# RWKV preparation: score and low-rank products issued in alternation over row halves and banks, key norms broadcast in one fp32r pass

## The chip, the core and the metric

The kernel runs on one core of a Trainium2 chip. Its metric is the device time of one execution in microseconds (us). The program is a whole small network, some 46,500 instructions long; the change touches one stage of it, about a sixth of the time.

Engines are called PE (TensorE, the matmul array), PEld (its weight loads), DVE (VectorE), ACT (ScalarE), POOL (GpSimd) and SP (SyncE, which here only issues transfers). Each engine runs its own instructions strictly in the order in which they were placed at build time; semaphores tie the engines together.

## The reference, cut to what matters

The network has two layers (attention with an mLSTM, then RWKV-7), two MLPs, a third mixer and a mixture of experts. The part that matters is the preparation of RWKV for 16 heads of 64 channels, 256 context tokens and 256 latent tokens:

```python
r, k, v = jnp.einsum('sbtd,sde->sbte', jnp.stack([xr, xk, xv]), w_rkv)
w_logit = w0 + einsum('zbtr,zrd->zbtd', tanh(einsum('btd,zdr->zbtr', xw, w1)), w2)   # z: two directions, r: 64
decay = exp(-exp(-softplus(-w_logit) - 0.5))
a = sigmoid(a0 + einsum('zbtr,zrd->zbtd', einsum('btd,zdr->zbtr', xa, a1), a2))
kk = split_heads(k * k_k);  kk = kk / max(norm(kk, axis=-1), 1e-12)       # one norm per token and head
k_dir = k[None] * (1.0 + (a - 1.0) * k_a)
...
return r, k_dir, v, decay, -kk, kk[None] * a, g
```

Then a state of 64 x 64 per head is scanned over the tokens, forward and backward (z = 0, 1). The kernel does the scan in chunks of 64 tokens: inside a chunk it needs the scores of every token against every earlier one, and the inverse of a unit triangular matrix made of them.

## The kernel before, in words

The RWKV layer (`layer1_mixer`) lies between about 860 and 1,500 us of the span. `rw_project` forms k, r, the low-rank tanh products `thw` and `tha` (rows 0 to 63 direction 0, rows 64 to 127 direction 1) and `rn`, the inverse key norms: 16 heads on 16 partitions by 512 tokens, from `rsqrt`.

After that the work runs in eight groups: context and latent segment, each with four groups `hq` of four heads. A group has two head pairs B (128 channels, one head per 64 partitions), and each pair two directions z; one (pair, direction) is called a unit below, so a group has four units and the stage 32. Group i goes through four steps:

- `rw_prep`: the elementwise coefficients of a unit (ACT and DVE), from the norms of its pair broadcast over 64 rows per head (L1261, the tile `pr`) and the low-rank products of its direction (L1271 with `w2`, L1272 with `a2`, one bank `pw` for the two). Then the scores of its two heads (L1319): `par` 0 has its operands on partitions 0 to 63, `par` 1 on 64 to 127, four chunks n each, with a masked copy to `sc` by DVE (L1322). Then four transposes (L1327) and their copy by ACT. Last, SP writes two 32 x 32 blocks per chunk to DRAM (L1332, `Ld`).
- `rw_solve`: a transfer reads `Ld` back as 128 rows (L1356, tile `L`), POOL (for group 1: DVE) inverts the triangles in 30 steps of two instructions (L1364, L1365), transfers write the result out (L1368) and back into `sc` (L1373). For groups 0 and 1 these transfers are on POOL's queue, for the others on SP's.
- `rw_merge`: joins 32-blocks to 64-blocks (L1385 transposes by DVE, L1390 and L1398 matmuls).
- `rw_scan`: four chunks in sequence, with matmuls that alternate between the directions (L1436 to L1483; L1453 has 64 x 64 operands, direction 0 on rows 0 to 63 and direction 1 on rows 64 to 127).

Groups are two ahead: the generator of `rw_prep` for group i + 2 is advanced between the chunks of `rw_scan` of group i, and `rw_solve` of group i + 2 is written after that scan. PE has two more kinds of work in the stage: the value projection (`v_product`, L242 to L244, before the first scan) and adaLN matmuls for the next block (`advance`, L337, with weights that SP loads into one buffer, L336).

The order on each engine isn't the order of the source. A scheduler at build time lists the instructions by its own estimates of their times and by when buffers come free, and each engine then keeps that order. PSUM in the stage: the tag `pa` has two banks, `pb` one, `s0` and `s1` two each for scans and merges, `ad` one. In the kernel before, `pa` serves `pr` and `pw`; `pb` serves the scores, the transposes and the coefficient product L1341.

An fp32 matmul shows in the trace as two records (a transpose or an fp32r matmul as one), each with its weight load. The operand shapes in the rows are rows*columns of the array in use, then the moving tile.

Of the kernel before, what the change touches and what calls it, by code (L numbers as in the profile page):

```python
# [23 lines left out]
F32 = mybir.dt.float32  # L24
FR = mybir.dt.float32r
I32 = mybir.dt.int32
U8 = mybir.dt.uint8
AF = mybir.ActivationFunctionType
OP = mybir.AluOpType
# [7 lines left out]
def bc(ap, shape):  # L37
    return ap.to_broadcast(shape)
# [12 lines left out]
class Kern:  # L51
# [115 lines left out]
    def put(self, parts, src, scale=None):  # L167
# [6 lines left out]
        else:  # L174
            nc.scalar.activation(h, src, AF.Copy, scale=scale)  # L175
            nc.vector.scalar_tensor_tensor(l, src, scale, parts[0], op0=OP.mult, op1=OP.subtract)  # L176

    def two(self, name, n, k, w):


        ts = [[self.big(name + i, k, w) for i in "hl"] for _ in range(n)]
        put = lambda b: tuple(t[:, b % k, :] for t in ts[b // k])
        return put, lambda b: tuple(v.bitcast(FR) for v in put(b))
# [67 lines left out]
    def setup(self):  # L251
        nc, tc, es = self.nc, self.tc, self.es
        self.cp = es.enter_context(self.pool("const", 1))
        cp = self.cp
        jp = cp.tile([128, 128], F32, name="jp")
        nc.gpsimd.iota(jp, pattern=[[1, 128]], base=0, channel_multiplier=-1, allow_small_or_imprecise_dtypes=True)
        self.ident = cp.tile([128, 128], F32, name="ident")
        nc.vector.tensor_scalar(self.ident, jp, 0.0, None, op0=OP.is_equal)
        self.negf = cp.tile([128, 128], F32, name="negf")
        nc.vector.tensor_scalar(self.negf, jp, 0.0, NEG, op0=OP.is_lt, op1=OP.mult)  # L260
        self.negb = cp.tile([128, 128], F32, name="negb")
        nc.vector.tensor_scalar(self.negb, jp, 0.0, NEG, op0=OP.is_gt, op1=OP.mult)
        self.jp = jp
        self.ones = cp.tile([128, 128], F32, name="ones")
        nc.vector.memset(self.ones, 1.0)


    def columns(self):
# [759 lines left out]
    def layer1_mixer(self):  # L1028
        nc, a = self.nc, self.a
        mc = self.modc[1]  # L1030
        with self.pool("rwp", 1) as P:
            rc = self.rw_consts(P)
            wr = a["rw_w_rkv"][0]
            w2 = P.tile([128, D], F32, name="rw_w2")
            nc.scalar.dma_start(w2, a["rw_w2"][0].rearrange("z r d -> (z r) d"))
            a2 = P.tile([128, D], F32, name="rw_a2")
            nc.scalar.dma_start(a2, a["rw_a2"][0].rearrange("z r d -> (z r) d"))
            thw = P.tile([128, 512], F32, name="thw")
            tha = P.tile([128, 512], F32, name="tha")
            rn = P.tile([16, 512], F32, name="rn")  # L1040

            S = P.tile([128, 16, 128], F32, name="rwS")
            nc.gpsimd.memset(S, 0.0)
# [55 lines left out]
    def rw_project(self, rc, mc, wr, w1, a1, g1, thw, tha, rn):  # L1099
        nc = self.nc  # L1100
# [5 lines left out]
        with self.pool("rwn", 2, side="right") as N:  # L1106
            for t in range(4):
                i = 1 if t < 2 else 0
# [3 lines left out]
        W = self.es_tmp.enter_context(self.pool("rwm", 2))  # L1112
# [34 lines left out]
        for n, wl, dst, fn in ((1, w1, thw, AF.Tanh), (4, a1, tha, AF.Copy)):  # L1147
            m = mix_all(n)
            p = self.ps("mm")
# [9 lines left out]
        m = mix_split(2)  # L1159
# [13 lines left out]
        for c in range(4):  # L1173
            wt = weights()
            for e in range(2):
                b = 2 * c + e
                p = self.ps("mm")
# [11 lines left out]
        for c in range(4):  # L1189
            wt = weights()  # L1190
            for e in range(2):
                p = self.ps("mm")
                for k in range(8):
                    self.matmul2(p[:, :256], tuple(x[:, e * 128:(e + 1) * 128] for x in wt(k)), m(k), k == 0, k == 7)
                if c + e == 0:
                    norms()
                    n2 = W.tile([16, 512], F32, name="kkn2", bufs=1)
                    nc.vector.tensor_scalar(n2, pn[:16], 1e-24, None, op0=OP.max)
                    self.rsqrt(W, rn, n2, 1.0, 0.0, "kkr")
                self.evac(rT[:, c * 2 + e, :], p[:, :256])  # L1200
        m = self.big("mix", 8, 256)
        for k in range(8):
# [32 lines left out]
    def rw_prep(self, W, rc, seg, hq, ar, w2, a2, thw, tha, rn, kT, rT, coef):  # L1235
# [21 lines left out]
        for b in range(2):  # L1257
            B = hq * 2 + b
            pr = self.ps("pa")
            for q in range(2):  # L1260
                nc.tensor.matmul(pr[q * 64:q * 64 + 64, :256], bc(self.ident[:16, 2 * B + q:2 * B + q + 1], [16, 64]),  # L1261
                                 rn[:, ts], start=True, stop=True)
            kkn = T("kkn")

            nc.vector.scalar_tensor_tensor(kkn, kT[:, B, :], rc["hkk"][:, B:B + 1], pr[:, :256],
                                           op0=OP.mult, op1=OP.mult)
            for z in range(2):
                zr = slice(z * 64, z * 64 + 64)
                rv = (lambda x: x) if z == 0 else (lambda x: x[:, ::-1])
                pw = self.ps("pa")  # L1270
                nc.tensor.matmul(pw[:, :256], w2[zr, B * 128:(B + 1) * 128], thw[zr, ts], start=True, stop=True)  # L1271
                nc.tensor.matmul(pw[:, 256:], a2[zr, B * 128:(B + 1) * 128], tha[zr, ts], start=True, stop=True)  # L1272
                lw, av = T("lw"), T("av")
                nc.scalar.activation(lw, pw[:, :256], AF.Tanh, scale=0.5, bias=rc["hw0"][:, z * 8 + B:z * 8 + B + 1])
                nc.scalar.activation(av, pw[:, 256:], AF.Tanh, scale=0.5, bias=rc["ha0"][:, z * 8 + B:z * 8 + B + 1])
# [36 lines left out]
                        nc.vector.tensor_add(cs, cs, kd[:, ::-1])  # L1312
                        self.rw_coef(rc, cs, B, coef)

                for par in range(2):
                    pr_ = slice(par * 64, par * 64 + 64)
                    p = self.ps("pb")
                    for n in range(4):
                        nc.tensor.matmul(p[:, n * NT:(n + 1) * NT], bkf[pr_, n].rearrange("p q s -> p (q s)"),  # L1319
                                         A[pr_, n, :], start=True, stop=True)  # L1320
                    u0 = z * 8 + par
                    nc.vector.tensor_mul(sc[b][:, u0:u0 + 7:2, :], p[:, :4 * NT].rearrange("p (n t) -> p n t", n=4),  # L1322
                                         bc(rc["mask"][:, z, None, :NT], [128, 4, NT]))
# [1170 lines left out]
```

## Time and profile before

| | us |
|---|---|
| median of 3 runs | 3162.48 |
| range of the runs | 3145.84 to 3168.23 |
| the profiled execution | 3164.53 |
| its span | 3162.8 |
| PE busy in the span | 2897.6 (92%) |
| DVE, ACT, POOL busy | 1500.9, 882.9, 460.1 |
| stage from the first norm broadcast to the end of the last scan | 978 to 1500 |
| mean granted TensorE clock | 0.925 |

Busy times of PE take in the modelled tail of each matmul. The chain of waits on the page follows only the last stage of the program (the experts), so the RWKV stage must be read from the trace by stretches. A granted clock of 1 is 2.4 GHz, of 0.5 is 1.2 GHz.

### The profile page before, as it was taken

Reading aid. Unit: us, or ns where it says so; the run is one execution under the profiler, and the core shown is the slowest. Engines: PE = TensorE matmul, PEld = TensorE weight load, DVE = VectorE, ACT = ScalarE, POOL = GpSimd, SP = SyncE. Lnnn points to the kernel's source line nnn. Section 1 sums busy time; section 2 is a strip of 40 time slices with the busy share of each in tenths; the row PEclk is TensorE's granted clock in tenths of the full one; section 3 lists DMA queues with packets and bytes.
Section 4 is the critical chain, followed back from the end, with each engine's and each line's share of the span. In section 5 each row is a group of like instructions: output and inputs, shape, how many; then the busy total and the mean of one; then the engine's idle time right before and its main releaser. Section 6 shows DMA issues by size and latency. Waiting matters only on the chain. (4 is left out here: it accounts for less than half of the span.)

```text
span 3162.8 us, 46512 instructions
## 1 busy us (share of the span) xinstructions
PE 2897.6 (92%) x18618; PEld 1840.2 (58%) x18618; DVE 1500.9 (47%) x3185; ACT 882.9 (28%) x1821; POOL 460.1 (15%) x714
## 2 busy tenths in 40 slices
PE   7999999999899999887999998999989998889987
PEld 4863568888757665554898866763433333333332
DVE  4436555555567557645656958551322222222122
ACT  4223343322334334323454624530000000000001
POOL 0012211111100434533101212110000000000000
PEclk9999999999997878878999968989999999999998
DMA  6326642333311234342555403368979999999994
GB/s 222 106 89 215 256 133 72 100 96 94 102 54 35 76 105 109 86 122 82 158 182 176 151 21 106 109 245 343 415 321 410 415 416 417 416 418 399 395 383 178
DMA packets 254000, 650.65 MB, mean 206 GB/s; under 512 B 68816, under 2 KB 129616, under 8 KB 215376
## 3 DMA queue, kind: packets, MB, share of 16 engines
q1 hardware_dynamic: 239552, 632.96, 54.4%
q10 hardware_dynamic: 12432, 10.45, 1.1%
q0 software_dynamic: 1792, 4.20, 0.5%
q8 instruction: 148, 2.42, 0.3%
q14 instruction: 76, 0.62, 0.1%
HBM read 639.16 MB, written 8.39 MB: 205 GB/s over the span
## 5 line engine op out<-in xcount | busy, mean ns | idle before, releaser
L2104 PE MATMUL mm<-w,xg 128*32 128x256 f32 (+1 forms) x3392 | 479.5, 486 | 0.9 <-DMA w<-in_moe_w_gu_dram 0.9
L164 DVE TENSOR_TENSOR lo<-w,hi 128x512 fp32r<-128x512 f32 (+1 forms) x330 | 297.0, 933 | 109.3 <-ACT hi L163 95.0
L163 ACT ACTIVATE hi<-w 128x512 fp32r<-128x512 f32 (+1 forms) x356 | 256.3, 770 | 235.4 <-PE tp L243 101.1
L2104 PEld LDWEIGHTS mm<-w,xg 128*32 128x32 f32 (+1 forms) x3392 | 158.7, 123 | 271.7 <-issue 232.9
L2104 PE MATMUL mm<-w,moeaT 128*32 128x256 f32 (+1 forms) x1696 | 262.9, 534 | 11.0 <-DVE moeaT L95 6.2
L2124 POOL TENSOR_TENSOR moeg<-moeg,moes 128x512 f32<-128x512 f32 (+1 forms) x39 | 41.8, 1072 | 960.4 <-ACT moes L2122 960.4
L2104 PEld LDWEIGHTS mm<-w,moeaT 128*32 128x32 f32 (+1 forms) x1696 | 90.1, 135 | 156.0 <-issue 123.1
L243 PE MATMUL mm<-mlo,hi 128*128 128x512 f32 (+1 forms) x512 | 173.3, 339 | 0.6 <-DVE mlo L173 0.6
L2147 DVE TENSOR_TENSOR moey<-mm,moegate 32x256 f32<-32x256 f32 (+1 forms) x106 | 58.0, 548 | 243.2 <-PE mm L2104 233.2
L242 PE MATMUL mm<-mhi,hi 128*128 128x512 f32 (+1 forms) x512 | 173.1, 340 | 0.0
L244 PE MATMUL mm<-mhi,lo 128*128 128x512 f32 (+1 forms) x512 | 172.3, 337 | 0.0
L2121 DVE TENSOR_SCALAR moeg<-mm 128x512 f32<-128x512 f32 (+1 forms) x39 | 23.2, 595 | 290.7 <-PE mm L2104 289.7
L2122 ACT ACTIVATE moes<-moeg 128x512 f32<-128x512 f32 (+1 forms) x39 | 21.6, 553 | 465.6 <-DVE moeg L2121 465.6
L244 PE MATMUL tp<-hi,aTl 128*128 128x512 f32 x384 | 151.6, 395 | 0.0
L243 PE MATMUL tp<-lo,aTh 128*128 128x512 f32 x384 | 151.4, 394 | 0.0
L242 PE MATMUL tp<-hi,aTh 128*128 128x512 f32 x384 | 151.0, 393 | 0.0
L164 POOL TENSOR_TENSOR lo<-w,hi 128x512 fp32r<-128x512 f32 (+1 forms) x26 | 52.8, 2032 | 370.9 <-ACT hi L163 316.5
L243 PEld LDWEIGHTS mm<-mlo,hi 128*128 128x128 f32 x512 | 96.4, 188 | 12.7 <-DVE mlo L173 1.0
L242 PEld LDWEIGHTS mm<-mhi,hi 128*128 128x128 f32 x512 | 96.0, 188 | 12.3 <-issue 0.2
L244 PEld LDWEIGHTS mm<-mhi,lo 128*128 128x128 f32 x512 | 96.4, 188 | 11.4
L1319 PE MATMUL pb<-ar,bkT 64*128 64x64 f32 (+1 forms) x512 | 96.6, 336 | 3.4 <-ACT bk L97 2.1
L2165 ACT ACTIVATE xg<-tp,modc,n 128x128 f32<-128x128 f32 x64 | 29.2, 457 | 241.2 <-DVE xg L2167 240.8
(843 smaller groups left out, 5921.1 us busy)
## 6 DMA issues: line engine op xcount, KB each, us to landing
w<-in_moe_w_gu_dram SPq DMA_DIRECT2D x256, 1024.0 KB, 17.4
w<-in_moe_w_down_dram SPq DMA_DIRECT2D x128, 1024.0 KB, 18.0
w<-in_mlp_w_dram SPq DMA_DIRECT2D x64, 1024.0 KB, 5.6
w<-in_ada_w_dram SPq DMA_DIRECT2D x48, 1024.0 KB, 5.2
w<-in_w_in_dram SPq DMA_DIRECT2D x26, 1024.0 KB, 5.3
adaw<-in_ada_w_dram SPq DMA_DIRECT2D x48, 512.0 KB, 4.1
w<-in_ab_w_in_dram SPq DMA_DIRECT2D x14, 1024.0 KB, 5.2
w<-in_rw_w_rkv_dram SPq DMA_DIRECT2D x8, 1024.0 KB, 5.3
```

The costliest lines, as they stand in the source:

```text
L163: nc.scalar.activation(h, raw, AF.Copy)
L164: (eng or nc.vector).tensor_sub(l, raw, hi)
L242: nc.tensor.matmul(out, l[0], r[0], start=start, stop=False)
L243: nc.tensor.matmul(out, l[0], r[1], start=False, stop=False)
L244: nc.tensor.matmul(out, l[1], r[0], start=False, stop=stop)
L1319: nc.tensor.matmul(p[:, n * NT:(n + 1) * NT], bkf[pr_, n].rearrange("p q s -> p (q s)"), A[pr_, n, :], start=True, stop=True)
L2104: return 8 * n, lambda p, c, l, r, s, st: nc.tensor.matmul(p[c * n:(c + 1) * n, :8 * n], l, r, start=s, stop=st, tile_position=(0, c * n))
L2121: nc.vector.tensor_scalar(g, pg[:, :w], 7.0, None, op0=OP.min)
L2122: nc.scalar.activation(s, g, AF.Sigmoid, scale=1.702)
L2124: nc.gpsimd.tensor_mul(g, g, s)
L2147: nc.vector.tensor_mul(y[:, cs], py[c * n:(c + 1) * n, :w], gate[c * n:(c + 1) * n, cs])
L2165: nc.scalar.activation(x[:, k, :], pv[:, kk, :], AF.Identity, scale=n2[:, k:k + 1], bias=sh(k))
```

## The change

There are three parts, all in the preparation.

1. **Scores.** The two heads of a unit get a bank each (`pb` for `par` 0, now `pa` for `par` 1), and the chunk loop is outside: the source alternates row half 0 and row half 1, chunk by chunk.
2. **Low-rank products.** Both directions' banks are taken at once (`pws`), and the four matmuls of a pair are written as w2 of direction 0, w2 of direction 1, a2 of direction 0, a2 of direction 1.
3. **Norms.** `rn` has 48 rows: a rounded part on rows 0 to 15, zeros, and the remainder on rows 32 to 47 (new helper `stack`, once). Per pair POOL spreads two columns of a constant into a 48 x 128 selector, and one fp32r matmul (L1274 of the changed kernel) makes both heads' rows. It takes the place of two fp32 matmuls of 16 rows by 64 columns.

```diff
+    def stack(self, t, rows):
+        nc = self.nc
+        nc.gpsimd.tensor_scalar(t.bitcast(FR), bc(self.ones[:48, 0:1], list(t.shape)), 0.0, None, op0=OP.mult)
+        nc.scalar.activation(t[0:16].bitcast(FR), rows, AF.Copy)
+        nc.vector.tensor_sub(t[32:48].bitcast(FR), rows, t[0:16])
...
+        self.two16 = cp.tile([48, 16], F32, name="two16")
+        nc.vector.tensor_add(self.two16.bitcast(FR), self.ident[:48, 0:16], self.ident[:48, 32:48])
...
-            rn = P.tile([16, 512], F32, name="rn")
+            rn = P.tile([48, 512], F32, name="rn")
...
-                    self.rsqrt(W, rn, n2, 1.0, 0.0, "kkr")
+                    self.rsqrt(W, n2, n2, 1.0, 0.0, "kkr")
+                    self.stack(rn, n2)
...
             pr = self.ps("pa")
-            for q in range(2):
-                nc.tensor.matmul(pr[q * 64:q * 64 + 64, :256], bc(self.ident[:16, 2 * B + q:2 * B + q + 1], [16, 64]),
-                                 rn[:, ts], start=True, stop=True)
+            sel = T("hsel", 128)[:48]
+            nc.gpsimd.tensor_scalar(sel.rearrange("p (q m) -> p q m", q=2).bitcast(FR),
+                                    bc(self.two16[:, 2 * B:2 * B + 2, None], [48, 2, 64]), 1.0, None, op0=OP.mult)
+            nc.tensor.matmul(pr[:, :256], sel.bitcast(FR), rn[:, ts].bitcast(FR), start=True, stop=True)
...
+            pws = [self.ps("pa") for _ in range(2)]
+            for i, (m, th) in enumerate(((w2, thw), (a2, tha))):
+                for z in range(2):
+                    zr = slice(z * 64, z * 64 + 64)
+                    nc.tensor.matmul(pws[z][:, i * 256:(i + 1) * 256], m[zr, B * 128:(B + 1) * 128], th[zr, ts],
+                                     start=True, stop=True)
             for z in range(2):
-                zr = slice(z * 64, z * 64 + 64)
...
-                pw = self.ps("pa")
-                nc.tensor.matmul(pw[:, :256], w2[zr, B * 128:(B + 1) * 128], thw[zr, ts], start=True, stop=True)
-                nc.tensor.matmul(pw[:, 256:], a2[zr, B * 128:(B + 1) * 128], tha[zr, ts], start=True, stop=True)
+                pw = pws[z]
...
-                for par in range(2):
-                    pr_ = slice(par * 64, par * 64 + 64)
-                    p = self.ps("pb")
-                    for n in range(4):
+                ps2 = [self.ps(tag) for tag in ("pb", "pa")]
+                for n in range(4):
+                    for par, p in enumerate(ps2):
+                        pr_ = slice(par * 64, par * 64 + 64)
                         nc.tensor.matmul(p[:, n * NT:(n + 1) * NT], bkf[pr_, n].rearrange("p q s -> p (q s)"),
                                          A[pr_, n, :], start=True, stop=True)
+                for par, p in enumerate(ps2):
                     u0 = z * 8 + par
```

The scheduler places the whole program anew, so the order on the engines changes beyond these lines, but, one small DVE instruction of the setup aside, only inside the RWKV stage. Three places follow. Lines of the changed kernel stand 10 to 17 lower in its source: L1335 is the score product, L1344 the transposes, L1284 the low-rank products, L1274 the norms, L249 to L251 the value projection.

On PE, the scores of the first unit, before: two runs of four matmuls into the one bank `pb`, with other work between.

```order
L1319 MATMUL pb<-ar,bkT 128x64 x4
L1261 MATMUL pa<-rn,ident 64x256 x2
L242 MATMUL s_7462<-hl,mix_6864 128x512
L243 MATMUL s_7462<-hl,mix_6864 128x512
L1319 MATMUL pb<-ar,bkT 128x64 x4
L244 MATMUL s_7462<-hl,mix_6865 128x512
```

The same unit in the changed kernel, with the matmul ahead of it and the transposes behind it:

```order
L251 MATMUL s_7471<-hl,mix_6870 128x512
L1335 MATMUL pb<-ar,bkT 128x64
L1335 MATMUL pa<-ar,bkT 128x64
L1335 MATMUL pb<-ar,bkT 128x64
L1335 MATMUL pa<-ar,bkT 128x64
L1335 MATMUL pb<-ar,bkT 128x64
L1335 MATMUL pa<-ar,bkT 128x64
L1335 MATMUL pb<-ar,bkT 128x64
L1335 MATMUL pa<-ar,bkT 128x64
L1344 MATMUL pb<-ident,bkT 128x128 x4
```

Here the eight matmuls alternate. 21 of the 32 units stand like this.

On PE, the fourth unit of the changed kernel (banks numbered; its scores are in `pa_7095` and `pb_7094`, `hsel` is the new selector):

```order
L1335 MATMUL pa_7054<-ar_6921,bkT_7046 128x64
L1335 MATMUL pa_7095<-ar_6921,bkT_7087 128x64 x2
L1344 MATMUL pb_7065<-ident_60,bkT_7046 128x128 x4
L1335 MATMUL pa_7095<-ar_6921,bkT_7087 128x64 x2
L1274 MATMUL pa_7198<-rn_5972,hsel_7199 128x256
L1335 MATMUL pb_7094<-ar_6921,bkT_7087 128x64 x4
L1284 MATMUL pa_7204<-thw_5970,rw_w2_5966 128x256
L1284 MATMUL pa_7205<-thw_5970,rw_w2_5966 128x256
```

Its two halves are not alternated: the half in `pa` goes ahead, around the third unit's transposes, and the half in `pb` follows. 11 units, all of direction 1, stand in this manner. The two directions' low-rank products stand next to each other.

On SP's queue, the read of group 4's blocks, before (`Ld_8902` is group 4's, `Ld_9480` group 5's):

```order
L1332 DMA Ld_8902<-sc_8900 32x8x32 x2
L336 DMA adaw_7702<-in_ada_w_2_dram 128x1024
L1332 DMA Ld_9480<-sc_9477 32x8x32
L1356 DMA L_9319<-Ld_8902 64x1024 x2
L1332 DMA Ld_9480<-sc_9477 32x8x32
```

and in the changed kernel (`Ld_8915` is group 4's, `Ld_9495` group 5's):

```order
L1349 DMA Ld_8915<-sc_8913 32x8x32 x4
L346 DMA adaw_7711<-in_ada_w_2_dram 128x1024 x2
L1373 DMA L_9334<-Ld_8915 64x1024 x2
L346 DMA adaw_7711<-in_ada_w_2_dram 128x1024
L1349 DMA Ld_9495<-sc_9492 32x8x32 x2
```

The read of group 4 stood behind a write of the next group's first unit; now it stands behind two adaLN loads. The same holds for group 5.

## Rows read from the trace of the kernel before

**Rows 1.** Page, part 1: busy time, share of the span, instructions of each engine.

```profile
PE 2897.6 (92%) x18618; PEld 1840.2 (58%) x18618; DVE 1500.9 (47%) x3185; ACT 882.9 (28%) x1821; POOL 460.1 (15%) x714
```

**Rows 2.** Stretches of the RWKV stage: length, busy time per engine, clock, DMA share, GB/s.

```profile
978.00:1018.00 40.00, 38.01 (x153) 26.61 (x150) 24.46 (x65) 15.62 (x43) 0.00 (x0) 0.66 0.05 12
1097.00:1142.00 45.00, 45.00 (x576) 29.95 (x575) 21.19 (x54) 20.46 (x53) 4.48 (x8) 0.81 0.36 106
1195.00:1244.00 49.00, 47.24 (x440) 28.56 (x440) 34.34 (x85) 17.43 (x44) 25.30 (x64) 0.76 0.35 91
1301.00:1360.00 59.00, 54.48 (x616) 36.50 (x614) 35.09 (x86) 18.97 (x49) 24.93 (x64) 0.82 0.30 76
1360.00:1500.00 140.00, 115.52 (x1526) 74.82 (x1522) 78.22 (x179) 49.15 (x117) 56.22 (x132) 0.83 0.35 101
```

**Rows 3.** Timeline of POOL: start, us, instruction, idle before and its releaser (solves).

```profile
1257.04 0.60 POOL L1358 COPY Tr<-L 64x512 f32<-64x512 f32 x1 [31.49 <-DMA L<-Ld]
...
1367.77 0.83 POOL L1358 COPY Tr<-L 64x512 f32<-64x512 f32 x1 [26.07 <-DMA L<-Ld]
...
1419.40 0.60 POOL L1358 COPY Tr<-L 64x512 f32<-64x512 f32 x1 [21.55 <-DMA L<-Ld]
...
1446.67 0.12 POOL L1367 MEMSET Tr<- 64x16 f32 x1
```

**Rows 4.** Timeline of SP's queue, around the read of group 4's blocks.

```profile
1243.47 0.89 SPq L1332 DMA_DIRECT2D Ld<-sc  x2
...
1252.19 2.20 SPq L1356 DMA_DIRECT2D L<-Ld  x2
```

**Rows 5.** Line L1385 (DVE, merges): what ended DVE's idle time (us, times).

```profile
  DMA sc<-Td: 15.5, 5
```

**Rows 6.** Timeline of PE: four score matmuls of one head, at either clock.

```profile
987.77 1.10 PE L1319 MATMUL pb<-ar,bkT 64*128 64x64 f32 x8 [0.21 <-DVE bkT L1301]
...
996.20 1.80 PE L1319 MATMUL pb<-ar,bkT 64*128 64x64 f32 x8
```

**Rows 7.** Timeline of PE: scan matmuls that alternate between the row halves.

```profile
1108.09 1.12 PE L1453 MATMUL s<-Xss,sc 64*64 64x64 f32 x16
```

**Rows 8.** Timeline of PE: low-rank products, one direction alone, then two together.

```profile
978.96 0.70 PE L1271 MATMUL pa<-thw,rw_w 64*128 64x256 f32 x2
979.49 0.59 PE L1272 MATMUL pa<-tha,rw_a 64*128 64x256 f32 x2
...
985.06 0.71 PE L1271 MATMUL pa<-thw,rw_w 64*128 64x256 f32 x4
985.59 0.61 PE L1272 MATMUL pa<-tha,rw_a 64*128 64x256 f32 x4
```

**Rows 9.** Timeline of PE: norm broadcast of a pair (x4) and of one head (x2).

```profile
978.38 0.65 PE L1261 MATMUL pa<-rn,ident 16*64 16x256 f32 x4
...
1002.24 1.11 PE L1261 MATMUL pa<-rn,ident 16*64 16x256 f32 x2
```

**Rows 10.** Timeline of PE: fp32r matmuls of 256 columns, back to back.

```profile
957.83 0.28 PE L242 MATMUL mm<-mix,hi 128*128 128x256 f32 x1
957.95 0.28 PE L243 MATMUL mm<-mix,hi 128*128 128x256 f32 x1
```

**Rows 11.** Groups on POOL, 1000 to 1460: busy us, mean ns, idle before.

```profile
L1364 POOL TENSOR_TENSOR Tm<-Tr,L 128x120 f32<-128x120 f32 x21 | 8.9, 426 | 1.6
```

**Rows 12.** Tile rn: duration ns min/median/max, first and last start us.

```profile
L115 DVE TENSOR_TENSOR rn<-rn,kkr_t x1: 678/678/678, 956.7 to 956.7; 16x512 f32<-16x512 f32 x1
```

**Rows 13.** Timeline of PE: value projection matmuls, back to back.

```profile
980.58 0.39 PE L244 MATMUL s<-hl,mix 128*128 128x512 f32 x1
980.81 0.40 PE L242 MATMUL s<-hl,mix 128*128 128x512 f32 x1
```

**Rows 14.** Line L1322 (DVE, masked copies): what ended DVE's idle time (us, times).

```profile
  PE pb L1319: 44.4, 39
```

**Rows 15.** Timeline of ACT: the first read of a `pw` bank.

```profile
980.12 0.48 ACT L1274 ACTIVATE lw<-pa,rw_hw 128x256 f32<-128x256 f32 x1 [1.26 <-PE pa L1272]
```

## The prediction

> **What bounds the kernel now.** I began with the page's first part: PE is busy for 92% of the span [rows 1]. That mean covers stages with other limits, and the page's chain covers only the experts, so I cut the RWKV stage into stretches. In four of them PE is busy for 38.01 of 40, 45.00 of 45, 47.24 of 49 and 54.48 of 59 us, while DVE has 21 to 35 us and the granted clock lies between 0.66 and 0.82 [rows 2]. These are the stretches in which the units of groups 0, 2, 4 and 6 are prepared.
>
> Between them something else paces. POOL idles before each solve until `L` lands: 31.49 us before group 4's, 26.07 before group 6's, 21.55 before group 7's [rows 3]. A solve takes about 27 us (1419.40 to 1446.67), and DVE in turn waits for the solved blocks to come back, 15.5 us in 5 waits [rows 5]. So I read one chain through the stage: PE prepares a group; its blocks go out and in by DMA; POOL solves; the blocks return; the merge starts; PE scans and prepares the group after next. The last links are solve 7, its merge and its scan, to 1500. From 1360 on PE is busy for 115.52 of 140 us [rows 2]. **PE time counts only where it lies in the four PE-paced stretches**; elsewhere it opens idle time that nothing asks for.
>
> **The change part by part.**
>
> *Scores.* Four matmuls of one head take 1.10 us at 2.4 GHz and 1.80 at 1.2 GHz [rows 6], some 0.2 of it the tail of the last; a unit has two such runs. What alternation does to them is not shown with this line, but nearly: the scan's 64-row matmuls that alternate between row halves finish 16 records in 1.12 us [rows 7], the time in which eight of the scores' finish. I take one run for the price of two: an alternated unit saves 0.9 us (1.10 less the tail) at the high clock and 1.7 at the low, 1.3 in a mixture. The bounds are nothing (the scan's pairs differ in columns too) and 1.8. By the order, 21 units alternate, of them three in group 0, three in group 2, two each in groups 4 and 6. For the other 11 I count nothing.
>
> *Low-rank products.* One direction takes 1.1 us (978.96 to the end of the second row), two that happen to stand together 1.14 (985.06 to the end of the fourth row) [rows 8]. That is the pattern of the change, already in the trace: the row halves run side by side. Saved per pair: 1.1 us at the high clock, about double at the low; where the trace paired them already, nothing. In program order those four instructions were w2, a2, w2, a2, yet the trace has all four w2 records before the a2 records. The Trainium skill's "TensorE: Matmul & The Clock Gate", section "Part 3: Packing small matmuls — row/col tiling", says that matmuls start and end strictly in program order; these rows disagree, two row halves do not wait for each other. By the page's rule only neighbours in the list would overlap; about half of this term would go, and the sum would be some 3 us less.
>
> *Norms.* A pair costs 0.65 us where its two matmuls stand together at the high clock, and twice 1.11 where they are apart at the low [rows 9]. One fp32r matmul of 256 columns costs 0.12, from start to start [rows 10], 0.24 at the low clock. Saved: 0.5 to 2.0 per pair. The selector is new on POOL; the nearest row is an operation of 128x120, 426 ns [rows 11]. Its 16 instances stand between or within the solves, at most one within each, so a solve gets at most 0.5 us longer (bounds 0 and 2 us per solve, if fp32r output is slow there). By the order they stand well ahead of their matmuls: the sixth pair's selector is made inside solve 0, its matmul comes in scan 0. The stacking of `rn` adds three operations, at most 2 us, before the first broadcast; `rn` is ready at 957.4 [rows 12] and first used at 978.38 [rows 9], so 21 us cover it. Without that cover it would cost its 2 us once.
>
> *Order.* The changed order puts 14 value-projection matmuls ahead of the first norm, at 0.23 us [rows 13] 3.3 us, where none stood. In group 4's stretch it puts 29 scan matmuls (58 records) more ahead of the last unit, at 1.12 us per 16 [rows 7] at most 4. On SP's queue, group 4's read was issued at 1252.19, 8.7 us after the group's last write at 1243.47 [rows 4], because a write of the next group stood between. Now two adaLN loads do, which wait for PE to free their buffer. Bounds 0 and 8; I take 4, the middle, as no row says how long these two wait.
>
> *The sum, along the chain.* Stretch of group 0 (clock falls to 1.2 GHz on the way): scores 0.9 + 2 x 1.7, low-rank 1.1 + 2.2, norms of the pairs up to there 0.5 + 0.5 + 0.5 + 2.0, less 3.3 for the order: 7.8. Group 2: scores 3 x 1.3, one pair's norm 2.0, low-rank 1.1: 7, of which I keep 6 as two products were paired already. Group 4: scores 2.6, norms 2.5, low-rank 1.5, less 3 to 4: 3. SP: 4. Group 6: scores 2.6, one norm 0.5, low-rank 1.1: 4. Together 25 us. What I charge at nothing: the preparations of groups 1, 3, 5 and 7 (covered by the solve and the transfers of the group before), the masked copies (unchanged in number), the tail, and all stages behind, which shift as a whole. If that cover fails, their savings count too (first rival). I keep the clock of each stretch as it is: nothing shows which way it would go.
>
> Against its own 3164.53 us the profiled execution would take **3139.5**. It lies 2 us above the median of the runs, 3162.48, so for the median I forecast **3137**, with 3122 to 3150 as this case's own range (each term by its bounds, not all at once).
>
> **The rivals.**
>
> *All of PE's saving counts.* If PE paces the stage throughout, as [rows 2] could also be read: scores 21 x 1.3 = 27, low-rank products about 14, norms 16 pairs at 1.1 = 17, less 3 for the order: 55 us, and the time is 3108. For it: DVE waits for the scores 44.4 us in 39 waits [rows 14]. Against it: POOL's idle times before the solves [rows 3].
>
> *Nothing but the queue.* PE's stretches shrink, but the units then follow the coefficients on ACT and DVE: DVE has 24.46 us for four units in the first stretch and 34.34 of 49 in the third [rows 2], and both engines follow one another within a unit. Then about a third of the 25 us stays, 8: 3154. "TensorEngine Tiling (Array Packing)" of the Trainium skill, section "PSUM Bottleneck", warns that tiling speeds up TensorE and not the evacuation. By that rule this rival would hold, and DVE's 60 to 70% in these stretches bears it out only in part. The same time results if row halves of different banks don't run side by side in the scores (the change then does not do what it says there), with norms and low-rank products alone gaining.
>
> *Slower: `pa` becomes the wait.* `pa` still has two banks, but now holds a norm, two products and half the scores. A score of direction 1 is listed ahead of the transposes of direction 0 in 11 units, as in the fourth; if its bank is still being read, PE stands before it, and behind it stand the transposes, the scan and the adaLN matmuls. ACT reads a `pw` bank in two steps of 0.48 us [rows 15]; with its queue ahead of it such a stop costs 2 to 4 us. All 32 units with 1.7 us each would cost 55, against 25 gained: 3192. It decides from 0.8 us per unit on. For it: banks were taken one at a time before. Against it: `pb`, which before took two scores and the transposes in turn in one bank, is relieved by as much.
>
> **How the numbers follow.** My forecast 0.45; all of PE's saving 0.20; a third of it 0.25; slower by `pa` 0.10. A difference under 1%, 31.6 us, can hardly be told from no change here, as the three runs span 22 us. Faster by over 1% means under 3131: the first rival whole and four tenths of the forecast (its term on SP's queue at 8, group 0's at its most), 0.38. Slower by over 1%, over 3194: half of the last rival, 0.05. Within 1%: the rest, 0.57. The range reaches from 3100, below the first rival's 3108, to 3172, which takes in the second rival and a slight loss; about 0.09 lies above it and 0.06 below.
>
> **What would show it.** In the profile of the changed kernel: an alternated unit's eight score matmuls in 1.1 to 1.2 us at 2.4 GHz; the low-rank products of a pair in about 1.15; one norm record per pair; the fourth unit's scores some 8 us earlier than now; the first solve on POOL earlier by as much; POOL's idle time before the solves kept or grown, since it is PE that got shorter; the last scan's end at about 1475. Waits of PE for ACT's `lw` or `av`, or for DVE's `sc`, before L1335 in direction 1 would be the last rival. The forecast is wrong in its main step if the distance from a merge to the end of the next group's preparation does not shrink, or if the solves move closer together by more than 15 us.

## The result, and the profile after

The changed kernel takes **3193.39 us** (median of 11 runs, 3175.31 to 3198.14), the kernel before 3158.57 beside it (11 runs): the ratio is **1.011, with a 95% interval of 1.0089 to 1.0131**. It is 35 us slower. The forecast was 3137 us, in a range of 3100 to 3172; the time lies above the range. What follows goes by a profiled execution with a span of 3195.7 us, against 3162.8 before.

The value projection lies 7 lines further on than in the rows of before, adaLN 10, the preparation, solves and merges 12 to 17; L95 and L97 are where they were: scores L1335, masked copies L1339, norm L1274, selector L1272, low-rank products L1284, `lw` and `av` on ACT L1290 and L1291, solve L1381 and L1382, adaLN L347, first merge matmul L1407.

Part 1 of the page, which answers to [rows 1]:

```profile
PE 2857.1 (89%) x18570; PEld 1818.1 (57%) x18570; DVE 1502.2 (47%) x3187; ACT 881.5 (28%) x1821; POOL 480.2 (15%) x731
```

PE has 40 us less to do, as was meant, and the span is 33 us longer. The time went into PE's idle time. The units tell where. One alternated unit in the timeline of PE (start, us, instruction), against [rows 6]:

```profile
1123.41 0.32 PE L1335 MATMUL pb<-ar,bkT 64*128 64x64 f32 x1
1123.41 0.32 PE L1335 MATMUL pa<-ar,bkT 64*128 64x64 f32 x1
1123.57 0.27 PE L1335 MATMUL pb<-ar,bkT 64*128 64x64 f32 x1
1123.58 0.27 PE L1335 MATMUL pa<-ar,bkT 64*128 64x64 f32 x1
...
1124.24 0.27 PE L1335 MATMUL pb<-ar,bkT 64*128 64x64 f32 x1
1124.24 0.27 PE L1335 MATMUL pa<-ar,bkT 64*128 64x64 f32 x1
```

The two heads run side by side: 16 records in 1.10 us, where one head's eight took as long before. So far the change does what it says. But the chain that followed from merge to preparation is longer, not shorter. From the start of a merge (first L1407) to the end of the last score of the group after next, in us:

```
                       before   changed
merge 0 to group 2       42.1      34.3
merge 2 to group 4       47.7      66.5
merge 4 to group 6       57.8      62.3
start of merge 7       1453.9    1475.7
last scan ends           1500      1529
```

Up to group 2 the forecast's gains are there: the fourth unit ends at 1011.8 instead of 1016.6, the twelfth at 1131.9 instead of 1139.4. Then it turns. What ended the engines' idle time between 1000 and 1440 us (us, times, longest), in the kernel before, four rows,

```profile
PE ad L337 <- DMA adaw<-in_ada_w_dram: 12.2, 3, 6.6
...
DVE Tn L1385 <- DMA sc<-Td: 14.6, 4, 6.1
...
DVE cum L1278 <- ACT lw L1276: 1.6, 2, 0.9
...
ACT lw L1274 <- PE pa L1272: 9.2, 6, 5.8
```

and in the changed kernel:

```profile
PE ad L347 <- DMA adaw<-in_ada_w_dram: 38.0, 7, 11.2
PE pb L1335 <- ACT E L1296: 12.4, 2, 6.6
...
DVE Tn L1402 <- DMA sc<-Td: 30.7, 7, 12.9
...
DVE cum L1294 <- ACT lw L1292: 19.1, 8, 4.0
...
ACT lw L1290 <- PE pa L1284: 12.9, 11, 3.2
...
POOL hsel L1272 <- PE pa L1274: 89.1, 6, 27.8
...
POOL hsel L1272 <- PE pa L1335: 23.4, 3, 14.2
```

Read them upwards along a unit: DVE waits for ACT's `lw`, ACT for PE's low-rank products, and PE before the scores for what ACT and DVE make of these. Before, DVE hardly ever waited for `lw`, and no wait of PE for `E` (ACT's exponentials) or `bkT` (DVE's last coefficient) stood ahead of the scores. Here is one unit, the 19th, in the timelines of the changed kernel, first PE:

```profile
1208.22 0.42 PE L1335 MATMUL pa<-ar,bkT 64*128 64x128 f32 x1
...
1212.50 1.05 PE L347 MATMUL ad<-adaw,s 128*32 128x512 f32 x4
1213.48 0.56 PE L1470 MATMUL s<-Xss,sc 64*64 64x64 f32 x10
...
1215.32 0.70 PE L1284 MATMUL pa<-thw,rw_w 64*128 64x256 f32 x4
1215.99 1.00 PE L1477 MATMUL s<-UVs,bk 128*64 128x64 f32 x16
1216.93 0.70 PE L1284 MATMUL pa<-tha,rw_a 64*128 64x256 f32 x4
...
1225.67 0.45 PE L1477 MATMUL s<-UVs,bk 128*64 128x64 f32 x2 [2.50 <-DVE UVs L95]
1226.05 0.58 PE L1335 MATMUL pb<-ar,bkT 64*128 64x128 f32 x1
1226.05 0.58 PE L1335 MATMUL pa<-ar,bkT 64*128 64x128 f32 x1
```

ACT,

```profile
1217.66 0.47 ACT L1290 ACTIVATE lw<-pa,rw_hw 128x256 f32<-128x256 f32 x1 [1.40 <-PE pa L1284]
```

and DVE:

```profile
1209.51 0.68 DVE L1339 TENSOR_TENSOR sc<-pa,rw_mask 128x512 f32<-128x512 f32 x1
...
1219.52 0.90 DVE L1294 TENSOR_TENSOR_SCAN cum<-rw_rs,lw 128x256 f32<-128x256 f32 x1
...
1225.45 0.41 DVE L1317 TENSOR_TENSOR bkT<-kd,E 128x256 f32<-128x256 f32 x1
```

The 18th unit's scores in `pa` end at 1208.6, DVE has read that bank at 1210.19, and only then, behind an adaLN step and a piece of the scan, come the low-rank products of the next pair. From their end at 1217.6 to the 19th unit's scores at 1226.05 the whole chain `lw`, `cum`, `E`, `bkT` runs with nothing ahead of it. Call this distance, from the end of a unit's low-rank products (of its pair's, where both directions are issued together) to the start of its scores, its **lead**. Over the 32 units its median is 49.3 us before (7.7 to 80.2) and 8.9 in the changed kernel (4.3 to 26.7). No row shown ahead of the forecast has this number; it takes the low-rank and the score rows of PE's timeline, unit by unit.

The second finding is on POOL. Two selectors in its timeline (with the idle time before each and its releaser), the first ahead of solve 3, the second in the middle of it:

```profile
1188.45 0.53 POOL L1272 TENSOR_SCALAR hsel<-two 48x128 fp32r<-48x128 f32 x1 [14.70 <-PE pa L1274]
...
1209.16 0.53 POOL L1272 TENSOR_SCALAR hsel<-two 48x128 fp32r<-48x128 f32 x1 [5.71 <-PE pa L1274]
```

A selector takes 0.53 us, near the 0.43 us of the row it was estimated from [rows 11]. But it has two buffers, and before it may write it waits until PE has read the selector of two pairs earlier. The 14.70 us ahead of solve 3 cost little, since the blocks for that solve had not come either (POOL waits 5.65 us more for `L`). The 5.71 us inside it hold it up: solve 3 takes 37.5 us instead of 28.3, of which wait and selector are 6.2.

### The profile page after: what moved, and what is told of

It is laid out like the page before. It is cut to its first block, busy times and chain, and to the rows that moved or that the text cites. A ratio compares the mean times of both kernels' runs of the same rounds, so it can differ in the third digit from the quotient of the medians.

```text
span 3195.7 us, 46466 instructions
## 1 busy us (share of the span) xinstructions
PE 2857.1 (89%) x18570; PEld 1818.1 (57%) x18570; DVE 1502.2 (47%) x3187; ACT 881.5 (28%) x1821; POOL 480.2 (15%) x731
## 5 line engine op out<-in xcount | busy, mean ns | idle before, releaser
L249 PE MATMUL mm<-mhi,hi 128*128 128x512 f32 (+1 forms) x512 | 173.1, 340 | 0.1
L251 PE MATMUL mm<-mhi,lo 128*128 128x512 f32 (+1 forms) x512 | 172.2, 337 | 0.0
L251 PE MATMUL tp<-hi,aTl 128*128 128x512 f32 x384 | 151.5, 395 | 0.0
L249 PE MATMUL tp<-hi,aTh 128*128 128x512 f32 x384 | 151.1, 393 | 0.0
L2139 ACT ACTIVATE moes<-moeg 128x512 f32<-128x512 f32 (+1 forms) x39 | 21.6, 553 | 468.1 <-DVE moeg L2138 468.1
L250 PEld LDWEIGHTS mm<-mlo,hi 128*128 128x128 f32 x512 | 96.3, 188 | 12.7 <-DVE mlo L173 1.0
L249 PEld LDWEIGHTS mm<-mhi,hi 128*128 128x128 f32 x512 | 96.0, 188 | 12.6 <-issue 0.5
L251 PEld LDWEIGHTS mm<-mhi,lo 128*128 128x128 f32 x512 | 96.4, 188 | 11.4
L249 PE MATMUL cv<-hT2h,hi 128*128 128x256 f32 x288 | 86.2, 300 | 9.3 <-DVE cvy L1754 9.2
## 6 DMA issues: line engine op xcount, KB each, us to landing
w<-in_moe_w_gu_dram SPq DMA_DIRECT2D x256, 1024.0 KB, 16.8
```

What stands on the lines that cost most here:

```text
L249: nc.tensor.matmul(out, l[0], r[0], start=start, stop=False)
L250: nc.tensor.matmul(out, l[0], r[1], start=False, stop=False)
L251: nc.tensor.matmul(out, l[1], r[0], start=False, stop=stop)
```

## The experiments

Times are medians; each ratio is to the kernel before, measured beside it, with its 95% interval. **The first theory** (A in the texts) was that the selectors on POOL do it; B is that two banks are too few for the new use of `pa`, C that the new order puts the adaLN loads worse on SP's queue. Four kernels did parts of the change alone.

**Scores alone**: only the hunk with `ps2` (two heads alternate, one in `pb`, one in `pa`).

> The kernel before with the scores alone changed: the two heads alternate between row halves, one head in pb, the other in pa. Norm broadcasts and low-rank products as before, no selector on POOL. Theory A (the selectors on POOL, which wait for PE to free their buffer in the middle of solves, cost the time): this part alone gains, 8 to 18 us against the kernel before, 3140 to 3150. Theory B (pa's two banks are over-asked by the changed use): slower by 5 to 20 us, with PE waiting before the scores of direction 1 for ACT's lw or av. Theory C (any new order puts the adaLN loads worse on SP's queue): no gain, within 5 us or slower, with PE waiting for adaw by 20 us or more between 1100 and 1440.

Measured: 3221.14, ratio 1.0224 (1.019 to 1.0258), 70 us slower. Theory A fell here: there is no selector in this kernel. B had 5 to 20 us and waits of PE for `lw` or `av`, of which there are none. C wanted PE to wait for `adaw` by 20 us or more, and it waits 14.0. The lead has a median of 7.2 us. DVE's wait for `lw` is more than twice that of the changed kernel:

```profile
DVE cum L1278 <- ACT lw L1276: 43.5, 19, 6.0
```

**Low-rank products alone**: only the hunk with `pws`.

> The kernel before with the low-rank products alone changed: both directions' products side by side, both pa banks taken at once. Theory A (selectors on POOL): gains 3 to 10 us, 3148 to 3155. Theory B (pa): slower by 5 to 25 us, since the norm of a pair and both its products now need three banks of two. Theory C (order on SP): within 5 us or slower, with adaw waits of 20 us or more on PE.

Measured: 3154.27, ratio 1.0021 (1.0001 to 1.004); lead 38.3. No gain, and a loss that is barely one.

**Norms alone**: the hunks with `stack`, `two16`, `sel`.

> The kernel before with the norms alone changed: one fp32r matmul per pair, with the selector made on POOL in two buffers and rn split in two. Theory A (selectors on POOL): slower by 25 to 50 us, 3183 to 3208; POOL waits for PE before hsel by 60 us or more between 1000 and 1440, solves 3 and 4 last 35 us or more. Theory B (pa): a gain of 3 to 10 us, since pa is held for shorter. Theory C (order on SP): slower only if PE waits for adaw by 20 us or more, wherever POOL stands.

Measured: 3165.45, ratio 1.0049 (1.0024 to 1.0073), 15 us slower; lead 51.3, and POOL waited for PE before `hsel` for 61.1 us in 6. Solve 3 takes 41.9 us with a wait of 12.7 inside it, solve 4 29.1. The direction of A is right, its size was not.

**Scores and low-rank products, without the norms.**

> The change without its norms: scores and low-rank products changed, norm broadcasts as before, no selector on POOL. Theory A (selectors on POOL): gains 12 to 25 us, 3133 to 3146. Theory B (pa): as slow as the whole change or slower, 3185 to 3210. Theory C (order on SP): 0 to 30 us slower with adaw waits of 20 us or more on PE.

Measured: 3168.53, ratio 1.0057 (1.0036 to 1.0078), 18 us slower; lead 8.6. PE waits for `adaw` 28.4 us, so by the letter C is met here, but not in the scores alone, which lose four times as much with half that wait. None of the theories had two parts that cost 70 and 4 us alone cost 18 together. The order in which `pa` is handed out explains it. Here are PE's records of the first pairs in order of time, n for norms, p for low-rank products, s for scores, with their number:

```
before              n4 p8 n4 p8 s8 n4 s8 p4 s16 p4 n4 s8 ...
scores alone        n4 p4 s16 p4 s16 n4 p4 s16 p4 s16 n4 ...
the change          n1 p8 s32 n1 p8 s21 n1 s10 p1 s1 p7 s21 ...
```

Before, products run ahead of the scores at once, and further later on. With the scores in `pa`, everything stands in the order of the source: tiles of one tag get their banks in turn, and a product whose turn comes after a score is not listed before it, however long its operands have been there. With the scores alone, the turn is norm, product 0, score 0, product 1, score 1, so each direction's products come after the scores of the unit before. In the change both products come first, and only the next pair's have to wait. That is less bad, as measured: the lead of direction 1's units has a median of 14.5 us here and 7.7 with the scores alone (direction 0: 6.4 and 7.0), and DVE's waits for `lw` halve in number, from 19 to 9:

```profile
DVE cum L1281 <- ACT lw L1279: 19.5, 9, 4.0
```

That is **theory R, the ring of `pa`**: the loss is that of the lead, and the lead is lost because scores and low-rank products take turns in one tag. It was put to test in four kernels.

**The bank alone, nothing alternated:**

```diff
-                    p = self.ps("pb")
+                    p = self.ps("pa" if par else "pb")
```

> The kernel before, with nothing changed but that the second head's scores take a bank of pa and not of pb; the matmuls stay one head after the other, nothing alternates. New theory R (the ring of pa): banks of a tag are given out in turn, so with scores in pa the low-rank products of the next unit must wait until the scores of an earlier one are read, and the 25 to 75 us by which the low-rank products run ahead of their scores in the kernel before shrink to 5 to 10; the loss of the scores' change is this alone. By R this kernel is slower than before by 60 to 100 us, at least as slow as the scores' change alone (3221), and the lead is 5 to 10 us from the third unit on. Rival A (alternating itself, or the order it gives on SP's queue, costs the time): within 10 us of the kernel before, lead 25 us or more.

Measured: 3228.16, ratio 1.0235 (1.0208 to 1.0262), 75 us slower, lead 7.2 (four units are above 10). The bank alone is as slow as the scores' whole change: the intervals of the two overlap, so whether alternating takes anything back can't be told from these. PE waits for `adaw` 16.8 us, little more than the 12.2 before. DVE's wait:

```profile
DVE cum L1278 <- ACT lw L1276: 48.9, 19, 6.9
```

**Both heads' scores in `pb`, one bank taken from `pa`** (scores alternated, the rest as before):

```diff
-            with self.psum(pa=2, pb=1, s0=2, s1=2, ad=1):
+            with self.psum(pa=1, pb=2, s0=2, s1=2, ad=1):
...
-                ps2 = [self.ps(tag) for tag in ("pb", "pa")]
+                ps2 = [self.ps(tag) for tag in ("pb", "pb")]
```

> Scores alternated as in the change, but both heads in banks of pb, which gets two; pa keeps one, for norms and low-rank products, which stay as before. The number of banks is the same. By theory R the scores no longer stand in the ring of the low-rank products, so the lead of these stays 15 us or more and the alternation's gain shows: 8 to 30 us faster than before, 3120 to 3143. Rival A (alternating or SP's order costs the time): slower than before by 30 us or more. Rival B (one bank for pa is too few): about the same as before or slower, with a lead under 12 us.

Measured: 3146.96, ratio 0.9968 (0.9947 to 0.9989), 6 us faster; lead 13.5. The same alternation, which came with a loss of 70 us when its second bank was one of `pa`, comes with none here. The gain is less than expected, with a lead between what R and rival B gave: one bank is little for norms and products.

**Two banks for each, one taken from the scan** (low-rank products paired, norms as before):

```diff
-            with self.psum(pa=2, pb=1, s0=2, s1=2, ad=1):
+            with self.psum(pa=2, pb=2, s=3, ad=1):
...
-            pX = self.ps(sx)
+            pX = self.ps("s")
```

(the same in every place of merge and scan; the value projection then takes three banks of `s` and one of `pb`).

> Scores alternated in two banks of pb, low-rank products of both directions side by side in two banks of pa, norms as before; the bank for it is taken from the scan, whose two tags of two banks become one of three. By theory R: lead 20 us or more, faster than before by 10 to 35 us, unless the scan waits for its banks: then PE waits for evacuations before the scan's matmuls grow by 20 us or more, and it is slower than the version with one bank for pa. Rival A: slower than before by 15 us or more.

Measured: 3133.21, ratio 0.9942 (0.992 to 0.9964), 20 us faster; lead 22.8.

**The selectors on ACT**, in the whole change:

```diff
-            nc.gpsimd.tensor_scalar(sel.rearrange("p (q m) -> p q m", q=2).bitcast(FR), ..., 1.0, None, op0=OP.mult)
+            nc.scalar.activation(sel.rearrange("p (q m) -> p q m", q=2).bitcast(FR), ..., AF.Copy)
```

(with three buffers instead of two).

> The whole change, but with the selectors made on ACT in three buffers, not on POOL in two. By the first theory (selectors that wait on POOL hold the solves): 10 to 20 us faster than the change, as the difference between it and its version without norms (3168.5 against 3193.4) is then the selectors' place; solves 3 and 4 in one piece, about 28 us each. By its rival (the norm's bank in pa costs it, not POOL): within 8 us of the change, though the solves are whole.

Measured: 3176.08, ratio 1.0065 (1.0036 to 1.0094), 23 us slower than before where the change is 35 slower. No selector stands in a solve any more, and solves 3 and 4 take 30.5 and 28.7 us instead of 37.5 and 36.0. So in the changed kernel the selectors' place and their two buffers (both were changed) cost about 12 us, an estimate from two measurements whose intervals just overlap; the lead, 9.1, stayed as it was.

The last four ask how much is the layout, how much the change.

**The layout alone** (the last `psum` line and nothing else of the change; `pb` with two banks takes the two heads one after the other):

> The kernel before with the bank layout alone of the faster version (two banks for pa, two for pb, three for the scan in one tag): the two heads' scores one after the other, low-rank products one direction at a time, norms as before. If alternating itself gains, this stays between the kernel before and the version with alternation (0.994 of before): 0.997 to 1.003. If the layout is all of that version's gain and alternating is worth nothing, this takes 0.992 to 0.996 of the time before. If three banks hold the scan up, over 1.003.

Measured: 3146.68, ratio 0.9964 (0.9941 to 0.9988), 10 us faster; lead 28.9. The intervals of this and of the version with alternated scores and paired products overlap, so that step alone, 10 us, is not told from nothing.

**The whole change in this layout**, selectors on POOL:

> The whole change, its selectors on POOL in two buffers, in the layout of the faster version: scores in two banks of pb, pa for norms and low-rank products alone. By theory R (the ring of pa): the lead comes back to 15 us or more and the time is faster than the change by 40 us or more, 3135 to 3160. With the selectors' price as found in the change (15 us), 10 to 20 us above the same version with selectors on ACT. If the selectors wait for less here, since norms run ahead, the two are within 6 us.

Measured: **3121.51, ratio 0.9894 (0.9869 to 0.9918), 35 us faster** than before and faster than the expected 3135 to 3160; lead 21.5. The only difference from the changed kernel is who gets which bank. What ended the idle time between 1000 and 1440:

```profile
DVE cum L1294 <- ACT lw L1292: 1.1, 1, 1.1
```

The low-rank products and the scores of its 19th unit on PE:

```profile
1169.90 0.59 PE L1284 MATMUL pa<-tha,rw_a 64*128 64x256 f32 x2
...
1190.42 0.38 PE L1335 MATMUL pb<-ar,bkT 64*128 64x128 f32 x2
```

The products are 20 us ahead again. From merge 0, 2 and 4 to the groups after next it is now 21.8, 28.5 and 41.6 us; merge 7 starts at 1402.8.

**The same with the selectors on ACT:**

> All three parts of the change in the layout of the faster version, the selectors on ACT in three buffers. By theory R and the selectors' price: 0.988 to 0.995 of the time before, 3115 to 3140, as fast as the version without the norms or up to 10 us faster. If the norms cost through pa's ring or by ACT's time (sixteen selectors at about 0.3 us): up to 8 us slower than that version.

Measured: 3119.91, ratio 0.9896 (0.9874 to 0.9917), the same. POOL still waits before `hsel` in the version above (22.3, 23.5 and 21.6 us in its three largest rows), but hardly inside a solve, where no wait is over 1.2 us. The price of a wait in an ordered list is that of its place.

**A third bank for `pa`, scores left in it:**

```diff
-            with self.psum(pa=2, pb=2, s=3, ad=1):
+            with self.psum(pa=3, pb=1, s=3, ad=1):
```

> The whole change with its scores left as they are, half in pb and half in the ring of pa, but that ring has three banks instead of two, again at the cost of one of the scan's four. The same number of banks in all as in the faster version (0.989), only the scores are still handed out in turn with the low-rank products. By theory R the turn still binds, one bank later: lead 10 to 25 us, and a time between that version and the change, 0.995 to 1.007 of the kernel before. If what the faster version gained were more banks for the preparation as such, whoever uses them: as fast as that version, 0.986 to 0.993.

Measured: 3186.34, ratio 1.0103 (1.007 to 1.0136); lead 9.2. More banks in the shared tag give nothing: as many banks as in the version at 0.9894, and the time of the change. I had expected that the third one takes back a part, and that was wrong: PE's order is again `n1 p8 s21 n1 ...` and `n1 p8 s32`, with no product further ahead than beside the last scores of the pair before. What binds with two banks and with three is the turn, not the number.

## Why the prediction was wrong

- **The step that failed gives the sign**: "PE time counts only where it lies in the four PE-paced stretches", with the units' coefficients on ACT and DVE put at nothing, as covered. PE could pace the stretches of groups 2, 4 and 6 because the low-rank products ran 24 to 80 us ahead of their scores there. The change gave that lead away, and the stretches of groups 4 and 6 became those of a chain through three engines: 66.5 us instead of 47.7, where 44.7 was forecast, and 62.3 instead of 57.8. The mark I had set for being wrong in the main step, this distance not shrinking, is met there. That the cause is the tag which scores and products share is shown: the bank alone loses 75 us, and the whole change with scores in `pb` gains 35. That the loss comes by way of the lead is read from the traces: it has a median of 7.2 to 9.2 us in all six kernels with scores in `pa`, which lose 18 to 75 us, and of 13.5 or more in the others. The median alone doesn't give the size of a loss, and the lead was never varied without the banks.
- **The rival with `pa` had the bank and the time (3192), not the mechanism.** It priced a stop of PE before the scores for ACT's `lw` or `av`; such waits are not among PE's. PE's order itself is different: the products stand behind the scores whose turn in `pa` comes first. "`pb` is relieved by as much", which spoke against it, was true and worth nothing, since no work ahead hung on `pb`. Its 1.7 us for each of 32 units came near the measured time by luck. Its chance of 0.10, with 0.05 for more than 1% slower, was too low.
- **The other two rivals.** *All of PE's saving counts* had 55 us; PE's busy time did fall by 40, and none of it came out of the time. *Nothing but the queue* named what took over, units that follow the coefficients on ACT and DVE, but let a third of the gain stay, with the chain of these engines starting as early as before; in fact it starts later. The share of DVE that its text gives as 60 to 70% is 47 to 70% by [rows 2].
- **The selectors**: "a solve gets at most 0.5 us longer" was wrong. I priced the operation and not its wait for its own buffer, though the text noted that it stands well ahead of its matmul, which is what makes it wait: up to 6.0 us inside a solve, with solve 3 9 us longer, and about 12 us in the time.
- **The row halves**: right. A unit's 16 records took 1.10 us, at a granted clock of 1.00 (1123 to 1125). The reading behind it compared across clocks, though: the scan's 1.12 us [rows 7] are from a stretch at 0.50 (1108 to 1110), the scores' 1.10 [rows 6] from one at 1.00 (985 to 989). For the low-rank products the first pair took 1.86 us (981.79 to 983.65) where 1.15 was forecast, one direction after the other: the norm had one of the two banks, and the second direction started at 982.53, when DVE had read it (982.47). Four records of one matrix took 0.70 later, as two did in [rows 8]. The Trainium skill's rule of strict program order ("TensorE: Matmul & The Clock Gate", "Part 3: Packing small matmuls — row/col tiling"), with which [rows 8] disagree, would have changed the term by 3 us and the result in nothing.
- **Groups 0 and 2**: near in size, 4.8 and 7.8 us where 7.8 and 6 were forecast. In group 0 this isn't the forecast's mechanism: from 978 to 1010 PE was busy for 21.97 us of 32, where it had been for 31.25, so it no longer paced the stretch. **SP's queue**: the solve of group 4 begins 10.1 us after that group's scores instead of 16.4, so the term of 4 was there, as 6.3. On the same queue, though, the loads for adaLN now stand behind blocks and solved triangles that come late:

```profile
1234.21 1.26 SPq L1385 DMA_DIRECT2D Td<-Tr  x2
1235.58 1.11 SPq L346 DMA_DIRECT2D adaw<-in_ada_w_dram  x2
...
1242.53 13.23 SPq L1349 DMA_DIRECT2D Ld<-sc  x4
1255.86 0.87 SPq L346 DMA_DIRECT2D adaw<-in_ada_w_dram  x2
```

  No adaLN weights are issued for 19 us, and PE waits for `adaw` 38.0 us in all against 12.2 before. With the lead restored it is 12.2 again. The two kernels that lose most, the bank alone and the scores alone, wait for it only 16.8 and 14.0 us, so it is not what the loss goes by; what it adds in the changed kernel was not tried alone.
- **The clock**: I kept each stretch's. Two windows of the changed kernel, then of the whole change in the other layout (length, busy time of PE, PEld, DVE, ACT, POOL, granted clock, DMA share, GB/s):

```profile
1200.00:1300.00 100.00, 80.23 (x765) 51.61 (x763) 56.36 (x133) 30.18 (x77) 51.57 (x121) 0.70 0.28 79
1300.00:1400.00 100.00, 83.79 (x964) 54.95 (x965) 61.55 (x151) 33.05 (x85) 40.32 (x97) 0.73 0.38 101
```

```profile
1200.00:1300.00 100.00, 93.83 (x1138) 59.00 (x1136) 80.78 (x198) 45.78 (x116) 56.12 (x136) 0.90 0.43 115
1300.00:1400.00 100.00, 84.09 (x1183) 55.78 (x1181) 51.63 (x128) 28.76 (x73) 49.35 (x136) 0.90 0.41 112
```

  Before, both had 0.82. The chain's stalls came with more time at the low level, which lengthens PE's share of it further. How much of the 35 us that is stays open.
- **In a layout that keeps the lead, the gain has the size of the forecast, by luck**: 25 us forecast, and the whole change takes 3121.51 there against 3146.68 for the layout alone, 25 us, with about 8 us either way in each (95%). It is not the same sum: there, more than half of it came with the norms, from 20 us faster than before (without them) to 35; the forecast had 8 to 9 of its 25 from them.

What stays open besides: why the low-rank products alone gained nothing. And of the 52 us by which the last scan ends earlier in the faster version (1448 against 1500), 35 are left at the end: behind the stage, up to the gates of the next mixer, PE has 1615 matmuls in 259 us instead of 1565 in 246. That is 13 of the 17 us that are missing; I take the 50 matmuls for work that stood beside the scan before; that isn't shown.

## What to carry to other kernels

Before a tile is moved to another PSUM tag, write down the tag's tiles in the order of their turns: if a tile at the end of a chain shares a tag with one at its start, the next round cannot begin before this one's end has had its turn. A third bank did not help here. An engine that is 95% busy may be so because others run far ahead of it; measure that lead (producer's end to consumer's start, unit by unit) and check that the change keeps it. And a small operation on an in-order engine can cost what its wait for a free buffer costs at its place in the list, and not its duration.

## What the runs showed of the hardware that was not expected

Matmuls on two row halves start together, not one after the other: pairs at 1123.41 and 1123.41, at 1226.05 and 1226.05, with the pairs 0.11 us apart at 64 columns and a granted clock of 1.00. So the sentence that each engine runs its instructions strictly in order does not hold between PE's row halves, as [rows 8] show already: of four products listed `w2`, `a2`, `w2`, `a2` the trace has all records of `w2` first, then those of `a2`. The scores were alternated in different banks only; the scan's pairs [rows 7] write one bank, on different partitions, and start together too. And the granted clock in a window did not follow PE's busy time there: 83.79 us of 100 went with 0.73 in the changed kernel, 84.09 with 0.90 in the faster one.
